# Later places for the transposes of the probabilities and the output products in a hybrid decoder layer

## The chip, the cores and the metric

The kernel runs on one core of a Trainium2 chip. The metric is the device time of one execution in microseconds, of which the median over several runs is compared. A profile of one execution shows every instruction of the engines: TensorE (PE, with its weight loads as PEld), VectorE (DVE), ScalarE (ACT), GpSimd (POOL) and SyncE (SP), which issues the weight transfers.

## The reference

One decoder layer on 256 positions of width 2048, all in float32. A projection gives a recurrent branch, a gating branch, 32 query heads on four key/value heads of size 64, and two merge gates. Attention looks at a window of 128 positions and has a sink in the denominator. After it come the merge, an output projection and an MLP of width 8192 with a squared ReLU. Cut to what matters here:

```python
h = rmsnorm(x, norm_mix_pre[l])
proj = h @ w_in[l]
xr, yr, q, k, v, g_rnn, g_attn = jnp.split(proj, IN_OFFSETS, axis=-1)
...
y_rnn = xr * jax.nn.gelu(yr)
q = rope(q.reshape(B, S, N_Q_HEADS, HEAD_DIM), positions)
k = rope(k.reshape(B, S, N_KV_HEADS, HEAD_DIM), positions)
y_att = sliding_window_sink_attention(q, k, v, attn_sinks[l])
mix = jax.nn.sigmoid(g_rnn) * (y_rnn @ w_rnn_proj[l]) + jax.nn.sigmoid(g_attn) * (y_att @ w_attn_proj[l])
x = x + rmsnorm(mix @ w_out[l], norm_mix_post[l])
h = rmsnorm(x, norm_mlp_pre[l])
u = jnp.square(jax.nn.relu(h @ w_mlp_up[l]))
x = x + rmsnorm(u @ w_mlp_down[l], norm_mlp_post[l])
...
# in the attention
m = jnp.maximum(jnp.max(scores, axis=-1, keepdims=True), sink)
p = jnp.exp(scores - m)
denom = jnp.sum(p, axis=-1, keepdims=True) + jnp.exp(sink - m)
probs = (p / denom).astype(v.dtype)
out = jnp.einsum('bnhgqk,bnkhd->bnqhgd', probs, vv)
```

## The kernel before, in words

**The weight stream.** All weights pass once, in one order, as halves of 128 x 1024 floats (`Stream`, L54). SyncE loads a half (L76), ScalarE casts it to a high part (`whi`, L94), VectorE subtracts to get the low part (`wlo`, L95), and TensorE makes float32 products from three products of parts. There are four raw buffers (`WRAW`) and six for each part (`WHALF`); a call of `ws.half()` splits up to six halves ahead, so the cast that it issues goes into the buffer of the half that TensorE has just finished.

**The passes.** `b_pass512` (L300) takes eight halves for one product of 256 rows by 512 columns: per half two steps, per step and row block three matmuls (L294, L296, L298), 12 matmuls a half and 96 a pass. `a_pair` (L243) takes four halves for two blocks of output channels, in turned form (L254, L256).

**The fill-in work.** Attention does not have a stage of its own. `waiting` is a list of generators; `pump()` (L227) resumes the first of them up to its next `yield`. `b_pass512` pumps after every `every` halves, `a_pair` four times in its four halves. So each `yield` in a generator marks one place among the matmuls of a pass.

**The order of the passes.** For each of four head groups g: a pass for the attention's merge gate (`g`, L646, which pumps after each half), then a pass for the queries (`q`, L648). The generator `attention(g)` (L532) is appended behind the query pass and so is resumed during the gate pass and the query pass of the next group; that of the last group during the first four `a_pair` passes of the recurrent branch (`recur(0)`, L765: two `conv`, two `gelu`), with `pump(99)` (L781) for what is left.

**The steps of `attention(g)`.** Rotary embedding of row block 0; transposes of the queries of block 0 and embedding of block 1; transposes of block 1; scores of both blocks, and the softmax of block 0; the softmax of block 1; `turn_probs(0)`; an empty step; `turn_probs(1)`; then the product with the values and its split into `yatt` (L626 to L635). `softmax(tb)` (L571) has nine exponentials on ScalarE (L578, L582, each of the latter followed by a row that reads its sum) and on VectorE a sum, a reciprocal and the division (L587), two instructions for block 0 and four for block 1. `turn_probs(tb)` (L592) makes two banks of four transposes for block 0 and four banks for block 1 (L604), each copied by ScalarE (L606). The pool `psm` from which these banks come has two. The product has 12 rows on TensorE (L630), two casts on ScalarE (L634) and two subtractions on VectorE (L635).

**What sets the order.** Within an engine a scheduler of the framework orders the recorded instructions; those under `pin` (the scores and the product matmuls) keep the program's order among themselves.

Of the kernel before, what the change touches and what calls it, by code (L numbers as in the profile page):

```python
# [28 lines left out]
TB = 2  # L29
# [137 lines left out]
def layer(tc, x, g_pre, pos_t, pos_row, inv_freq, vecs, sinks, gains, w_kv, w_q, w_xy, w_rg, w_g, w_rp, w_ap, w_out,  # L167
# [43 lines left out]
    def unit(name, dt=F32R):  # L211
        return big.tile([P, 4, 2, S], dt, tag="U8", name=name)

    def flat(t):
        return t.rearrange("p a b c -> p (a b c)")
# [3 lines left out]
    def units(name):  # L219
        return [unit(f"{name}{i}") for i in range(4)]  # L220

    def bank(pool, name):
        return pool.tile([P, 512], F32, tag=pool.name, name=name)

    waiting = []

    def pump(n=1):  # L227

        for _ in range(n):
            while waiting:  # L230
                try:
                    next(waiting[0])
                    break
                except StopIteration:
                    waiting.pop(0)
# [50 lines left out]
    def b_step(banks, acts, kt, hi, lo, last, tbs=(0, 1)):  # L286

        a = acts[kt // 4][:, kt % 4]
        first = kt == 0
        nb = len(banks[tbs[0]])  # L290
        for tb in tbs:
            t = slice(tb * P, tb * P + P)
            for n in range(nb):
                mm(banks[tb][n], a[:, 0, t], hi[:, n * 512 : n * 512 + 512], start=first, stop=False)  # L294
            for n in range(nb):
                mm(banks[tb][n], a[:, 0, t], lo[:, n * 512 : n * 512 + 512], start=False, stop=False)  # L296
            for n in range(nb):
                mm(banks[tb][n], a[:, 1, t], hi[:, n * 512 : n * 512 + 512], start=False, stop=last)  # L298

    def b_pass512(acts, banks, every=2):  # L300

        for j in range(8):
            hi, lo = ws.half()
            for i in range(2):
                c = slice(i * 512, i * 512 + 512)
                b_step([[b] for b in banks], acts, 2 * j + i, hi[:, c], lo[:, c], 2 * j + i == KT - 1)
            if (j + 1) % every == 0:
                pump()
        return banks

    def two_banks(name):
        room = pair(name)
        return [room[:, tb].rearrange("p a b -> p (a b)") for tb in range(TB)]
# [7 lines left out]
    psb = ctx_ps.enter_context(tc.tile_pool(name="psb", bufs=2, space=bass.MemoryType.PSUM))  # L321
# [45 lines left out]
    hT = units("hT")  # L367
# [164 lines left out]
    def attention(g, banks):  # L532
# [38 lines left out]
        def softmax(tb):  # L571
            stat = stats[tb]
            w = P * (1 + tb)
            per = 512 // w
            nc.vector.tensor_tensor(stat[:, 0, :], stat[:, 0, :], sk, ALU.max)
            nc.vector.tensor_scalar(stat[:, 1, :], stat[:, 0, :], -1.0, None, ALU.mult)
            nc.vector.tensor_tensor(stat[:, 2, :], sk, stat[:, 1, :], ALU.add)
            nc.scalar.activation(stat[:, 2, :], stat[:, 2, :], AF.Exp)  # L578
            for s3, at in tiles[tb]:
                for i in range(per):  # L580
                    c = slice(at + i, at + i + 1)
                    nc.scalar.activation(s3[:, i, :], s3[:, i, :], AF.Exp, bias=stat[:, 1, c],  # L582
                                         accum_out=stat[:, 3, c])
            nc.vector.tensor_tensor(stat[:, 2, :], stat[:, 2, :], stat[:, 3, :], ALU.add)
            nc.vector.reciprocal(stat[:, 2, :], stat[:, 2, :])
            for s3, at in tiles[tb]:
                nc.vector.tensor_tensor(s3, s3, stat[:, 2, at : at + per].unsqueeze(2).to_broadcast([P, per, w]),  # L587
                                        ALU.mult)
# [3 lines left out]
        def turn_probs(tb):  # L592
            nk = 1 + tb
            per = 4 // nk
            if tb:
                room_p = flat(unit("pT", F32)).rearrange("p (n c) -> p n c", c=512)
            else:
                room_p = rooms[tb][:, 2:4, :]
            for par in range(2):
                for kb in range(nk):  # L600
                    ps = bank(psm, "pt")
                    for h in range(4):
                        s3, at = tiles[tb][h // per * 2 + par]
                        nc.tensor.transpose(ps[:, h * P : h * P + P], s3[:, h % per, kb * P : kb * P + P], ident)  # L604
                    t = room_p[:, par * nk + kb, :]
                    nc.scalar.copy(t, ps)  # L606
                    pT[tb, par, kb] = t
# [9 lines left out]
        if last_group:  # L617
            scores(1, 1, [bank(psb, "sc") for par in range(2)])
        softmax(1)
        yield  # L620
        turn_probs(0)
        yield
        yield
        turn_probs(1)
        yield
        for tb in range(TB):  # L626
            po = bank(psm, "po")
# [16 lines left out]
    for g in range(NKV):  # L644
        m1.append(pa.tile([P, TB, 512], F32, tag="m1", bufs=4, name=f"m1{g}"))
        for tb, b in enumerate(b_pass512(hT, two_banks("g"), 1)):  # L646
            nc.scalar.activation(m1[g][:, tb], b, AF.Tanh, scale=r0h[tb])
        waiting.append(attention(g, b_pass512(hT, [bank(psb, f"q{tb}") for tb in range(TB)])))  # L648


    lam = vec[:, 7, :]
# [182 lines left out]
    psb = ctx2.enter_context(tc.tile_pool(name="psb2", bufs=4, space=bass.MemoryType.PSUM))  # L834
# [166 lines left out]
    for tb in range(TB):  # L1001
        for i in range(2):
            q = 2 + i
# [145 lines left out]
    for f in range(2):  # L1149
# [3 lines left out]
        for p in range(PAIRS):  # L1153
# [11 lines left out]
            if f == 1 or p >= R2_AT:  # L1165
                for q, u in full:
                    if q in SEVEN:
                        uT[q] = pc.tile([P, 2, 7, P], F32R, tag="seven", bufs=len(SEVEN), name=f"seven{f}{q}")
                    else:
                        i = sum(k not in SEVEN for k in range(q))  # L1170
# [137 lines left out]
```

## Time and profile before

| | |
|---|---|
| median of three runs | 1514.89 us |
| lowest and highest run | 1511.7 and 1516.5 us |
| span of the profiled execution | 1515.7 us |
| mean granted TensorE clock | 0.998 |
| transposes of the probabilities (L604), all groups | 96 rows, 14.13 us busy between 97 and 292 us |
| stage of the gate and query passes and `recur(0)` | about 45 to 298 us |

The page gives no time of the profiled execution beyond its span. The rows of a timeline give start and length in microseconds, engine, line, operation, the tiles written and read, the shape, how many equal instructions are merged, and in brackets the idle time of that engine before the row and what ended it. Lengths of matmuls overlap their successors, so costs on TensorE are read from start to start. `pt` is a bank of transposed probabilities, `s` the room of scores and probabilities, `po` the bank of the product, `q`, `g` and `ps` the banks of the passes.

### The profile page before, as it was taken

Reading aid. Unit: us, or ns where it says so; the run is one execution under the profiler, and the core shown is the slowest. Engines: PE = TensorE matmul, PEld = TensorE weight load, DVE = VectorE, ACT = ScalarE, POOL = GpSimd, SP = SyncE. Lnnn points to the kernel's source line nnn. Section 1 sums busy time; section 2 is a strip of 40 time slices with the busy share of each in tenths; the row PEclk is TensorE's granted clock in tenths of the full one; section 3 lists DMA queues with packets and bytes.
Section 4 is the critical chain, followed back from the end, with each engine's and each line's share of the span. In section 5 each row is a group of like instructions: output and inputs, shape, how many; then the busy total and the mean of one; then the engine's idle time right before and its main releaser. Section 6 shows DMA issues by size and latency. Waiting matters only on the chain.

```text
span 1515.7 us, 20016 instructions
## 1 busy us (share of the span) xinstructions
PE 1493.5 (99%) x7600; PEld 1259.8 (83%) x7600; DVE 1102.2 (73%) x1377; ACT 829.2 (55%) x1143; POOL 5.5 (0%) x11
## 2 busy tenths in 40 slices
PE   9999999999999999999999999999999999999996
PEld 7787778788888888888888888888888888888875
DVE  6666677858769966555667866798886666688897
ACT  6554654646566766443355655555454455555543
POOL 0000000000000000000000000000000000000001
PEclk9999999999999999999999999999999999999999
DMA  6645445465646565655764756566657555566564
GB/s 253 218 144 187 142 131 170 153 196 166 217 159 215 174 209 196 191 183 194 268 225 137 271 183 193 185 203 213 219 195 239 194 188 188 193 236 213 195 209 174
DMA packets 82895, 296.19 MB, mean 195 GB/s; under 512 B 9712, under 2 KB 9968, under 8 KB 81648
## 3 DMA queue, kind: packets, MB, share of 16 engines
q1 hardware_dynamic: 79056, 284.43, 57.4%
q10 hardware_dynamic: 3744, 10.50, 1.9%
q8 instruction: 59, 0.97, 0.2%
q14 instruction: 36, 0.29, 0.1%
HBM read 288.60 MB, written 6.29 MB: 195 GB/s over the span
## 4 chain that ended last, share of the span: by engine, by line
PE 82%; DVE 9%; DMA 4%; ACT 2%; issue 2%; DVEq 0%; SPq 0%; ACTq 0%
PE ps L256 21%; PE ps L254 11%; PE dQ L1084 4%; DMA wraw<-in_w_dn 4%; PE pp L294 4%; PE pp L296 4%; PE pp L298 4%; PE g L294 3%; DVE wlo L95 3%; PE g L298 3%; PE g L296 3%; PE s L1084 3%; PE dP L1084 2%; PE q L296 2%; PE q L298 2%; PE q L294 2%
## 5 line engine op out<-in xcount | busy, mean ns | idle before, releaser
L94 ACT CAST whi<-wraw 128x1024 fp32r<-128x1024 f32 x523 | 544.6, 1053 | 567.5 <-PE ps L256 123.7
L95 DVE TENSOR_TENSOR wlo<-wraw,whi 128x1024 fp32r<-128x1024 f32 x523 | 632.8, 1221 | 301.9 <-ACT whi L94 295.2
L256 PE MATMUL ps<-h2T,whi 128*128 128x512 f32 x960 | 223.9, 390 | 0.0
L256 PEld LDWEIGHTS ps<-h2T,whi 128*128 128x128 f32 x960 | 178.2, 188 | 35.6
L256 PE MATMUL ps<-hT,whi 128*128 128x512 f32 x512 | 121.3, 391 | 0.0
L254 PEld LDWEIGHTS ps<-h2T,wlo 128*128 128x128 f32 x960 | 119.1, 192 | 2.3
L254 PE MATMUL ps<-h2T,wlo 128*128 128x256 f32 x960 | 119.9, 283 | 0.0
L256 PEld LDWEIGHTS ps<-hT,whi 128*128 128x128 f32 x512 | 94.7, 188 | 20.1 <-issue 1.5
L1084 PE MATMUL dQ<-whi,uT 128*128 128x512 f32 x288 | 106.9, 389 | 0.0
L294 PE MATMUL g<-whi,hT 128*128 128x512 f32 x256 | 101.2, 395 | 0.0
L296 PE MATMUL g<-wlo,hT 128*128 128x512 f32 x256 | 100.0, 391 | 0.1
L298 PE MATMUL g<-whi,hT 128*128 128x512 f32 x256 | 99.8, 390 | 0.0
L254 PE MATMUL ps<-hT,wlo 128*128 128x256 f32 x512 | 64.9, 283 | 0.0
L254 PEld LDWEIGHTS ps<-hT,wlo 128*128 128x128 f32 x512 | 63.8, 191 | 1.2
L1084 PEld LDWEIGHTS dQ<-whi,uT 128*128 128x128 f32 x288 | 54.1, 188 | 11.2
L1084 PE MATMUL dQ<-wlo,uT 128*128 128x512 f32 x144 | 56.4, 391 | 1.2 <-DVE wlo L95 1.1
L294 PEld LDWEIGHTS g<-whi,hT 128*128 128x128 f32 x256 | 48.1, 188 | 10.6 <-issue 1.0
L298 PEld LDWEIGHTS g<-whi,hT 128*128 128x128 f32 x256 | 48.1, 188 | 10.2
L296 PEld LDWEIGHTS g<-wlo,hT 128*128 128x128 f32 x256 | 48.1, 188 | 9.9 <-DVE wlo L95 0.5
L1084 PE MATMUL dCs<-whi,uT 128*128 128x512 f32 x144 | 54.1, 389 | 0.0
L1084 PE MATMUL dP<-whi,uT 128*128 128x512 f32 x144 | 54.1, 389 | 0.0
L130 DVE TENSOR_TENSOR tlo<-t,thi 128x1536 fp32r<-128x1536 f32 x28 | 49.2, 1756 | 5.5 <-ACT thi L129 5.3
(280 smaller groups left out, 2462.1 us busy)
## 6 DMA issues: line engine op xcount, KB each, us to landing
wraw<-in_w_up SPq DMA_DIRECT2D x128, 512.0 KB, 4.1
wraw<-in_w_dn SPq DMA_DIRECT2D x128, 512.0 KB, 4.8
wraw<-in_w_g SPq DMA_DIRECT2D x64, 512.0 KB, 4.7
wraw<-in_w_xy SPq DMA_DIRECT2D x64, 512.0 KB, 4.5
wraw<-in_w_q SPq DMA_DIRECT2D x32, 512.0 KB, 4.4
wraw<-in_w_ap SPq DMA_DIRECT2D x32, 512.0 KB, 4.6
wraw<-in_w_rp SPq DMA_DIRECT2D x32, 512.0 KB, 4.1
wraw<-in_w_out SPq DMA_DIRECT2D x32, 512.0 KB, 4.9
```

The source lines that it names most:

```text
L94: self.pin(self.nc.scalar.copy(hi, src))
L95: self.pin(self.nc.vector.tensor_tensor(lo, src, hi.bitcast(F32), ALU.subtract))
L130: v.tensor_tensor(lo, t, hi.bitcast(F32), ALU.subtract)
L254: mm(ps[:, f, 1, :], w, a[:, 0, :], start=False, stop=j == 1 and k == 7)
L256: mm(ps[:, f].rearrange("p a b -> p (a b)"), w, a.rearrange("p a b -> p (a b)"), start=kt == 0, stop=j == 3 and k == 7)
L294: mm(banks[tb][n], a[:, 0, t], hi[:, n * 512 : n * 512 + 512], start=first, stop=False)
L296: mm(banks[tb][n], a[:, 0, t], lo[:, n * 512 : n * 512 + 512], start=False, stop=False)
L298: mm(banks[tb][n], a[:, 1, t], hi[:, n * 512 : n * 512 + 512], start=False, stop=last)
L1084: mm(b, a[x], w[y], start=not begun and i == 0, stop=tail and i == 2)
```

## The change

In `attention`, four more empty steps stand between the softmax of block 1 and `turn_probs(0)`, and one more between `turn_probs(1)` and the product. The query pass pumps after each half and no longer after every second one.

```diff
@@ -617,11 +617,13 @@
         if last_group:
             scores(1, 1, [bank(psb, "sc") for par in range(2)])
         softmax(1)
-        yield
+        for i in range(5):
+            yield
         turn_probs(0)
         yield
         yield
         turn_probs(1)
+        yield
         yield
         for tb in range(TB):
             po = bank(psm, "po")
@@ -645,7 +647,7 @@
         m1.append(pa.tile([P, TB, 512], F32, tag="m1", bufs=4, name=f"m1{g}"))
         for tb, b in enumerate(b_pass512(hT, two_banks("g"), 1)):
             nc.scalar.activation(m1[g][:, tb], b, AF.Tanh, scale=r0h[tb])
-        waiting.append(attention(g, b_pass512(hT, [bank(psb, f"q{tb}") for tb in range(TB)])))
+        waiting.append(attention(g, b_pass512(hT, [bank(psb, f"q{tb}") for tb in range(TB)], 1)))
```

In steps of the list above: `turn_probs(0)` was the sixth resumption of a group's generator and is the tenth, `turn_probs(1)` was the eighth and is the twelfth, and the product was the ninth and is the fourteenth. In halves of weights: the two turns come four halves later, the product four later in groups 0 to 2 (from behind the second half of the query pass to behind the sixth) and five later in the last group (from the third `a_pair` pass into the fourth).

## The prediction

> **What bounds the kernel now.** I read the page's head first, then the windows by stage, then the waits of TensorE, and only then the timeline around the transposes of the probabilities.
>
> ```profile
> span 1515.7 us, 20016 instructions
> PE 1493.5 (99%) x7600; PEld 1259.8 (83%) x7600; DVE 1102.2 (73%) x1377; ACT 829.2 (55%) x1143; POOL 5.5 (0%) x11
> PE 82%; DVE 9%; DMA 4%; ACT 2%; issue 2%; DVEq 0%; SPq 0%; ACTq 0%
> ```
>
> TensorE is busy for 1493.5 of 1515.7 us, and 82% of the chain that ended last is TensorE's. A microsecond in which TensorE stands still in the middle of the program is therefore a microsecond of the total, unless a later stage takes it back. The windows (start and end, length, then busy time and count of TensorE, weight loads, VectorE, ScalarE, GpSimd, granted clock, DMA share, GB/s) show where it stands still:
>
> ```profile
> 176.00:215.00 39.00, 39.00 (x196) 32.01 (x195) 25.93 (x38) 15.39 (x24) 0.00 (x0) 1.00 0.55 168
> 215.00:231.00 16.00, 14.57 (x76) 9.93 (x75) 10.45 (x16) 14.52 (x39) 0.00 (x0) 1.00 0.41 129
> 292.00:800.00 508.00, 508.00 (x2543) 432.45 (x2542) 341.83 (x394) 279.49 (x354) 0.00 (x0) 1.00 0.61 199
> 1322.00:1500.00 178.00, 175.88 (x786) 144.42 (x785) 150.81 (x148) 90.95 (x94) 3.81 (x2) 1.00 0.63 212
> ```
>
> From 176 to 215 us and from 292 to 800 us nothing is lost. The 16 us in which group 2 turns its probabilities lose 1.43 us. The last down projection, 1322 to 1500 us, loses 2.12 us. The view of waits, for TensorE alone, names the loss in the attention (total, times, longest):
>
> ```profile
> PE pt L604 <- DVE s L587: 4.4, 3, 1.5
> ```
>
> The transposes wait for the division of the softmax (L587) on VectorE. Group 1 in the timeline of TensorE (start, length, what, idle before it); the gap from one start to the next is what counts, since the lengths overlap:
>
> ```profile
> 160.97 0.39 PE L294 MATMUL q<-whi,hT 128*128 128x512 f32 x1
> 162.78 1.23 PE L604 MATMUL pt<-ident,s 128*128 128x128 f32 x8 [1.42 <-DVE s L587]
> 163.76 0.47 PE L296 MATMUL q<-wlo,hT 128*128 128x512 f32 x1
> 164.07 0.39 PE L298 MATMUL q<-whi,hT 128*128 128x512 f32 x1
> ...
> 169.13 0.39 PE L298 MATMUL q<-whi,hT 128*128 128x512 f32 x1
> 169.36 1.03 PE L604 MATMUL pt<-ident,s 128*128 128x128 f32 x8
> 170.15 0.48 PE L294 MATMUL q<-whi,hT 128*128 128x512 f32 x1
> ```
>
> A projection matmul takes 0.23 us from start to start (169.13 to 169.36), eight transposes that wait for nothing take 0.79 (169.36 to 170.15), and the first matmul behind transposes takes 0.31 (163.76 to 164.07), 0.08 more than its fellows; I call that the return. Against this the first turn stands 1.81 us behind the one matmul ahead of it, which is 1.58 too many, and its eight take 0.98, 0.19 too many, because the second four wait for the second division. Together 1.77 us in this group.
>
> **The change part by part.** It puts the 24 transposes, six copies, twelve product matmuls, two casts and two subtractions of each group later among the matmuls of the next pass. It adds and removes none of them, issues no DMA, and in the changed program SyncE's queue has the order that it had. On TensorE the order for groups 0 to 2 becomes: 24 matmuls of the query pass, the eight transposes of block 0, 24 matmuls, eight of block 1, three matmuls, the other eight (in groups 1 and 2 as four, one matmul, four), some 20 matmuls, the product. The more frequent call from the query pass alone moves nothing else, since no other generator waits then.
>
> *The waits removed.* VectorE and ScalarE in group 1:
>
> ```profile
> 161.94 1.29 DVE L587 TENSOR_TENSOR s<-s,stat 128x512 f32<-128x512 f32 x2
> 165.98 2.50 DVE L587 TENSOR_TENSOR s<-s,stat 128x512 f32<-128x512 f32 x4
> 168.40 1.22 DVE L95 TENSOR_TENSOR wlo<-wraw,whi 128x1024 fp32r<-128x1024 f32 x1
> ...
> 165.41 1.05 ACT L606 COPY s<-pt 128x512 f32<-128x512 f32 x2
> 166.35 1.05 ACT L94 CAST whi<-wraw 128x1024 fp32r<-128x1024 f32 x1
> 167.31 1.26 ACT L647 ACTIVATE m<-g,st 128x512 f32<-128x512 f32 x2
> 168.46 1.06 ACT L606 COPY pT<-pt 128x512 f32<-128x512 f32 x2
> ```
>
> The divisions end at 163.23 and 168.48, that is 2.3 and 7.5 us after the query pass begins at 160.97. In the changed order block 0 is turned after 24 x 0.23 = 5.5 us and block 1 after 48 x 0.23 and the 0.87 of the first turn with its return, 11.9 us. Both divisions are over by 3 to 4 us, so the waits go in full. The same count for the others, first groups 0 and 2, then the last group, whose turns stand in the paired passes of the recurrence:
>
> ```profile
> 108.60 0.39 PE L294 MATMUL q<-whi,hT 128*128 128x512 f32 x1
> 109.06 1.23 PE L604 MATMUL pt<-ident,s 128*128 128x128 f32 x8
> 110.04 0.48 PE L296 MATMUL q<-wlo,hT 128*128 128x512 f32 x1
> ...
> 216.01 0.39 PE L294 MATMUL q<-whi,hT 128*128 128x512 f32 x1
> 217.83 1.23 PE L604 MATMUL pt<-ident,s 128*128 128x128 f32 x8 [1.43 <-DVE s L587]
> ```
>
> ```profile
> 268.38 1.32 PE L256 MATMUL ps<-hT,whi 128*128 128x512 f32 x5
> 271.25 0.63 PE L604 MATMUL pt<-ident,s 128*128 128x128 f32 x4 [1.54 <-DVE s L587]
> ...
> 272.30 0.48 PE L256 MATMUL ps<-hT,whi 128*128 128x512 f32 x1
> ...
> 278.31 2.19 PE L254 MATMUL ps<-hT,wlo 128*128 128x256 f32 x17
> 280.60 0.63 PE L604 MATMUL pt<-ident,s 128*128 128x128 f32 x4
> 280.99 0.96 PE L254 MATMUL ps<-hT,wlo 128*128 128x256 f32 x6
> 281.81 0.63 PE L604 MATMUL pt<-ident,s 128*128 128x128 f32 x4
> 282.19 0.84 PE L254 MATMUL ps<-hT,wlo 128*128 128x256 f32 x5
> 282.89 1.15 PE L604 MATMUL pt<-ident,s 128*128 128x128 f32 x8
> 283.79 0.72 PE L254 MATMUL ps<-hT,wlo 128*128 128x256 f32 x4
> ```
>
> Group 0: 0.46 - 0.23 = 0.23 before and 0.19 inside, 0.42, and 0.04 because two fours with two returns become one eight with one: 0.46. Group 2: 1.82 - 0.23 + 0.19 = 1.78. Last group: 2.87 us for five matmuls, 1.72 too many. Then 1.05 us for eight transposes and a matmul, against 0.79 + 0.31 in one piece: 0.05 worse. Then 17 short matmuls in 2.29 us, where six and a return take 0.82, so 0.12 each and 2.04 for 17: 0.25 too many. Last 0.39 + 0.38 + 0.90 and three returns, 1.91, against two eights and two returns, 1.74: 0.17. Together 2.09. The sum over the groups is 0.46 + 1.77 + 1.78 + 2.09 = 6.1 us.
>
> *The waits added.* The block-1 turn needs four banks and the pool has two, so its third bank waits for the copy of the first. Before, that copy stood right behind TensorE, which was the late one. In the changed order of groups 1 and 2 a cast of a weight half (L94) stands ahead of the copies on ScalarE, and this cast waits for the buffer that TensorE gives free with its 48th matmul, just ahead of the turn. Let P be the turn's start. The 48th matmul starts 0.23 earlier and is 0.39 long, so the cast starts at about P + 0.2, the next instruction follows 0.96 later (166.35 to 167.31), and the first copy (1.06 for two, 0.59 for one) ends at P + 1.74. TensorE wants the bank at 0.79 + 0.31 + 2 x 0.23 = P + 1.56. A release reached TensorE 0.20 us after the first division (161.94 + 0.64 to 162.78); for a copy I take 0.1 to 0.2. That is a wait of 0.3 us in each of the two groups. Is ScalarE there in time? Behind its last exponential at 165.41 stand cast, two tanh, two casts, two copies, two casts: 0.96 + 1.15 + 1.92 + 0.94 + 1.92 = 6.9, to 172.3. P is 160.97 + 11.9 = 172.9, and the last cast is released at 173.1. It is, by 0.8 us. In group 0 a different cast order leaves the copies free, and nothing waits. In the last group the copy of the pass that has just ended stands ahead:
>
> ```profile
> 271.91 1.26 ACT L606 COPY s<-pt 128x512 f32<-128x512 f32 x2 [2.81 <-PE pt L604]
> ...
> 274.66 0.59 ACT L283 COPY px<-ps 128x512 f32<-128x512 f32 x1 [0.54 <-PE ps L256]
> ```
>
> With such a copy of 0.48 start to start ahead, the bank copies end at about P + 1.3 and P + 1.75, while TensorE wants them at 1.1 and 1.8 plus any wait: 0.4 us. Added in all: 0.3 + 0.3 + 0.4 = 1.0. Bounds: nothing, if the copies come in time; 1.0 plus a cast of 0.96 in three groups, 3.9, if ScalarE is late.
>
> The row at 271.91 shows ScalarE idle for 2.81 us for the transposes with a cast right behind it, so it took its instructions in order. [...]
>
> *Costed at nothing.* The product moves with its 2.7 us. Its copies and casts lie beside projection matmuls on ScalarE and VectorE, which have 1.5 and 5.5 us free in the 16 us of group 2 above. The weight halves stay ahead: the low part of the query pass's fifth half is made at 168.40 and over at 169.6, and without the stalls TensorE would want it behind the second turn's first eight, at about 172.9 + 0.8 = 173.7, 4 us later; if that cover went, TensorE would wait there instead. Attention products of the last group end inside the fourth paired pass, and their first reader wants that group's share only in the seventh of eight halves that follow, some 16 us on.
>
> *The sum.* 6.1 - 1.0 = 5.1 us. The profiled execution's span of 1515.7 becomes 1510.6. No time around the span is given for it; the span lies 0.8 above the median of the runs, 1514.89 (1511.7 to 1516.5). From the median: **1509.8**.
>
> **The rivals.**
> A gain of at least 0.3%, 4.54 us, is about what a measurement of this kernel can tell from no change: below 1510.35 is faster, above 1519.43 slower.
>
> *The copies come in time.* The third bank is never late. For it: ScalarE's 0.8 us in hand. Against: the cast is tied to TensorE's 48th matmul. Time: 1514.9 - 6.1 = 1508.8.
>
> *ScalarE is a cast late.* The exponentials hold ScalarE longer than counted, so in three groups the bank copies come 0.96 later: 6.1 - 3.9 = 2.2, so 1512.7. For it: the reserve is only 0.8 us. Against: the same instructions ran at this pace before.
>
> *The last stage takes it back.* If weights there arrive at a pace of their own, 1514.9 remains. For it: the 2.12 us lost from 1322 to 1500, where VectorE is busy 150.81 of 178. Against: nothing there starts before TensorE's release of a buffer, so the stage should move as a whole.
> [...]
>
> *A half late, slower.* If a bank copy stands behind a cast whose buffer is free only after a half that itself stands behind the waiting transposes, TensorE and ScalarE wait in turn, and each group loses about a half: 12 x 0.23 = 2.8 us, 11.0 in all, against 6.1 gained: 1519.8. It decides from 10.6 / 4 = 2.65 us per group. Against: the casts ahead of the copies are released by matmuls that stand ahead of the transposes.
>
> **How the numbers follow.** Forecast 0.60, its own range 1508.5 to 1512 by the bounds above and the scatter of the runs, of which 0.42 lies below 1510.35 and 0.18 above. Copies in time 0.18, faster. A cast late 0.10 and the last stage 0.05, both within 0.3%. A half late 0.07, of which 0.06 slower and 0.01 within. So faster 0.60, same 0.34, slower 0.06. The range 1506.0 to 1514.5 takes in the copies in time with 3 us of scatter below, the forecast and the late cast; the last two cases are left out.
>
> **What would show it.** In the changed profile TensorE's wait for the division (4.4 us in three times) is gone, and the matmul ahead of block 0's turn is followed at 0.23. Waits of the third transpose bank for the copies show 0.3 to 0.4 in groups 1, 2 and the last. Windows over the same instructions are shorter by 0.46, 1.5, 1.5 and 1.7 us. The prediction is wrong if these windows shrink and the span does not, if TensorE waits for a low part in the query passes, or if the bank waits exceed a cast.

## The result, and the profile after

The changed kernel is slower. Its median is 1518.86 us (1515.52 to 1522.69, 13 runs) beside 1514.73 for the kernel before (1511.7 to 1516.5, 13 runs): a ratio of 1.0026 with a 95% interval of 1.0019 to 1.0034, 4.1 us more. That is inside the 0.3% that the text ahead called no change, but the interval leaves no doubt of the sign. 1509.8 was forecast, and the range ended at 1514.5.

The head of the page of the changed kernel, and its chain of waits by engine:

```profile
span 1520.9 us, 20016 instructions
PE 1494.9 (98%) x7600; PEld 1262.8 (83%) x7600; DVE 1101.0 (72%) x1377; ACT 829.3 (55%) x1143; POOL 5.5 (0%) x11
PE 89%; DVE 5%; DMA 3%; ACT 2%; issue 1%; SPq 0%; DVEq 0%; ACTq 0%
```

The same 7600 matmuls keep TensorE busy as long as before to within 1.4 us, so most of the time came as waits, not as work. The profiled execution took 1522.69 us, 1.8 more than its span, and is the slowest of its runs; that is why lengths of stretches are compared below, and medians for the whole. The view of waits for TensorE (total, times, longest) has one row of the transposes left:

```profile
PE pt L604 <- ACT pT L606: 9.3, 4, 3.7
```

The wait for the division, 4.4 us in three times, is gone. In its place the transposes wait for the copies that empty their banks, 9.3 us. The timeline of TensorE in group 1 of the changed kernel shows one such place:

```profile
172.63 0.39 PE L298 MATMUL q<-whi,hT 128*128 128x512 f32 x1
172.86 1.03 PE L604 MATMUL pt<-ident,s 128*128 128x128 f32 x8
...
174.20 0.40 PE L298 MATMUL q<-whi,hT 128*128 128x512 f32 x1
178.30 0.66 PE L604 MATMUL pt<-ident,s 128*128 128x128 f32 x4 [3.71 <-ACT pT L606]
...
181.20 0.63 PE L296 MATMUL q<-wlo,hT 128*128 128x512 f32 x1
181.63 0.63 PE L298 MATMUL q<-whi,hT 128*128 128x512 f32 x1
...
185.75 1.08 PE L632 MATMUL po<-s,v_sb 128*64 128x512 f32 x4
```

Block 1's turn starts at 172.86 behind its predecessor by 0.23 us, without a wait, just where the prediction put it (172.9). Then its third bank comes 4.1 us after the matmul ahead of it. ScalarE over the same stretch:

```profile
167.59 1.99 ACT L94 CAST whi<-wraw 128x1024 fp32r<-128x1024 f32 x2
169.48 1.07 ACT L606 COPY s<-pt 128x512 f32<-128x512 f32 x2
170.43 1.06 ACT L94 CAST whi<-wraw 128x1024 fp32r<-128x1024 f32 x1
173.66 1.05 ACT L94 CAST whi<-wraw 128x1024 fp32r<-128x1024 f32 x1 [2.17 <-DMA wraw<-in_w_g]
176.72 1.04 ACT L94 CAST whi<-wraw 128x1024 fp32r<-128x1024 f32 x1 [2.01 <-DMA wraw<-in_w_g]
177.67 1.07 ACT L606 COPY pT<-pt 128x512 f32<-128x512 f32 x2
```

The bank copies, ready to run from about 173.5, stand behind two casts that each wait some 2 us for a weight half which is still on its way. In the kernel before, the same copies ran at 168.46 and 170.35, and in the view of ScalarE's waits from 155 to 190 us no cast there is held last by a load: its casts wait for TensorE to free a buffer, 2.2 us at the longest. Why the halves are late is in the chain of waits of the changed kernel (start, length, what):

```profile
164.61 0.99 ACT s L582 x4
165.60 0.94 ACT whi L94
166.54 1.05 ACT m L649 x2
...
167.59 2.00 ACT whi L94 x2
...
169.62 1.22 DVE wlo L95
...
170.86 5.76 DMA wraw<-in_w_g
...
176.72 1.04 ACT whi L94
177.76 0.49 ACT pT L606
```

Read it backwards: the copy waited for a cast, the cast for a load of 5.76 us, the load for a raw buffer, the buffer for the low part that VectorE made at 169.62, and this for the second of the two casts that ScalarE began at 167.59, behind its exponentials (L582, over at 165.6), another cast and two tanh (L649). Of the two late loads the chain goes through the second alone. SyncE's queue in the kernel before shows that the pause was there already (start, length from the first issue to the last, count):

```profile
146.35 13.57 SPq L76 DMA_DIRECT2D wraw<-in_w_q  x4
169.64 17.99 SPq L76 DMA_DIRECT2D wraw<-in_w_g  x8
```

Between 160 and 169.6 us no weight half is requested (in the changed kernel until 169.7): all four raw buffers are full, because the softmax holds the two engines that empty them; 9.6 us is SyncE's longest wait for a low part in either kernel between 150 and 175 us. So the pause is old; the change moved the copies from before its consequences to behind them.

The windows of the changed kernel (start and end, length, busy time and count of TensorE, weight loads, VectorE, ScalarE, GpSimd, clock, DMA share, GB/s) add one thing:

```profile
172.80:178.30 5.50, 1.79 (x12) 1.25 (x10) 2.03 (x3) 2.63 (x4) 0.00 (x0) 1.00 0.88 285
178.30:187.00 8.70, 8.70 (x35) 6.42 (x37) 2.01 (x3) 3.80 (x6) 0.00 (x0) 0.80 0.40 142
```

Behind the stall the granted clock is 0.80 over these 8.70 us (0.50 in a window from 179 to 182 us), and the matmuls at 181.20 and 181.63 follow each other by 0.43 us, not 0.23. The stall's price has a second part that no wait shows.

To set kernel against kernel I measured four stretches of TensorE, each from the first matmul of one pass to the first of a later one, over the same instructions: the query pass behind group 0, 1 and 2 each, and the recurrent branch with the last group. For group 1 that is 160.97 to 190.20 before and 161.05 to 194.07 changed.

| stretch, us | before | changed | difference |
|---|---|---|---|
| group 0 | 27.92 | 28.57 | +0.65 |
| group 1 | 29.23 | 33.02 | +3.79 |
| group 2 | 29.24 | 32.91 | +3.67 |
| last group | 56.58 | 55.74 | -0.84 |
| sum | | | +7.27 |

### The profile page after: what moved, and what is told of

It reads as the page before. It is cut to its first block, busy times and chain, and to the rows that moved or that the text cites. A ratio compares the mean times of both kernels' runs of the same rounds, so it can differ in the third digit from the quotient of the medians.

```text
span 1520.9 us, 20016 instructions
## 1 busy us (share of the span) xinstructions
PE 1494.9 (98%) x7600; PEld 1262.8 (83%) x7600; DVE 1101.0 (72%) x1377; ACT 829.3 (55%) x1143; POOL 5.5 (0%) x11
## 4 chain that ended last, share of the span: by engine, by line
PE 89%; DVE 5%; DMA 3%; ACT 2%; issue 1%; SPq 0%; DVEq 0%; ACTq 0%
PE ps L256 22%; PE ps L254 12%; PE dQ L1086 7%; PE pp L294 4%; PE pp L296 4%; PE pp L298 4%; PE s L1086 4%; PE g L294 4%; PE g L296 4%; PE g L298 4%; PE dP L1086 3%; PE dCs L1086 2%; DMA wraw<-in_w_dn 2%; PE o L296 2%; PE o L298 2%; PE o L294 2%
## 5 line engine op out<-in xcount | busy, mean ns | idle before, releaser
L256 PE MATMUL ps<-h2T,whi 128*128 128x512 f32 x960 | 223.9, 390 | 0.0
L256 PEld LDWEIGHTS ps<-h2T,whi 128*128 128x128 f32 x960 | 178.2, 188 | 35.6
L256 PE MATMUL ps<-hT,whi 128*128 128x512 f32 x512 | 121.0, 391 | 0.0
L256 PEld LDWEIGHTS ps<-hT,whi 128*128 128x128 f32 x512 | 94.7, 188 | 19.4 <-issue 0.7
```

The lines of the kernel that those rows point to most:

```text
L256: mm(ps[:, f].rearrange("p a b -> p (a b)"), w, a.rearrange("p a b -> p (a b)"), start=kt == 0, stop=j == 3 and k == 7)
```

## The experiments

The theory: the gain in the turns is real, and it is lost because block 1's third and fourth bank wait for copies that stand on ScalarE behind casts that wait for late loads (ready from about 173.5, the first pair in group 1 began at 177.67). The rivals: the loss comes from the products or the weight halves (the low part, or the half itself, late for TensorE), from the later last stage, or from the turn's position as such. Ratios are against the kernel before in runs beside it.

**Four banks for block 1 in the query passes.** The copies stay where they are behind the casts, but TensorE no longer needs them inside the turn:

```diff
+            more = two_banks("pt") if tb and not last_group else None
...
-                    ps = bank(psm, "pt")
+                    ps = more[kb] if more and par else bank(psm, "pt")
```

with the four copies issued behind the four banks.

> The changed kernel, with the places of all steps kept, but in groups 0 to 2 the four banks of block 1's transposes come from two pools (two banks of the small pool, two of a pair that is free in the query pass), so no transpose waits for a copy of an earlier one. Queue theory (the copies stand on ScalarE behind casts that wait for a weight half's landing, and TensorE waits for the copies): the waits of TensorE for these copies (9.3 us in the changed kernel) fall under 1 us, the granted clock in groups 1 and 2 stays at 1.00, the stretch from query pass to next pass falls from 33.0 to about 27.7 us in each of the two, and the median falls by 9 to 11 us to 1508 to 1510. Starvation theory (the weights themselves are late, and TensorE would stand still a little later in any case): the wait moves to the weight loads or low parts of the halves that follow, and the median stays at 1516 to 1519.

Measured: 1508.72 us beside 1513.72, a ratio of 0.9965 (0.9952 to 0.9977). The stretches are 27.40, 27.42, 27.42 and 55.78: 4.95 us less than before in sum. ScalarE of this kernel in group 1, and TensorE's turn:

```profile
172.94 1.04 ACT L94 CAST whi<-wraw 128x1024 fp32r<-128x1024 f32 x1 [2.19 <-DMA wraw<-in_w_g]
175.11 1.05 ACT L94 CAST whi<-wraw 128x1024 fp32r<-128x1024 f32 x1 [1.13 <-DMA wraw<-in_w_g]
176.07 2.04 ACT L615 COPY pT<-pt 128x512 f32<-128x512 f32 x4
```

```profile
172.10 1.91 PE L607 MATMUL pt<-ident,s 128*128 128x128 f32 x16
173.76 0.48 PE L294 MATMUL q<-whi,hT 128*128 128x512 f32 x1
```

The casts still wait for the loads, and the copies still come 4 us after the turn's start; but all 16 transposes run in one piece and nobody waits. So neither products nor weight halves nor the position are the loss: it is that the turn has two banks while their copies are late. The last group, which has two banks in this kernel too, keeps one wait of 1.1 us for a copy.

**The second turn one half earlier.** One `yield` instead of two between the turns, three instead of two behind the second.

> The changed kernel with the turn of block 1 one weight half behind that of block 0 instead of two, and the product one later, so that it stays where it was put. Queue theory: one cast fewer, or two, stands ahead of the copies, and the last of these needs no load that was held up by the softmax; TensorE's waits for the copies fall from 9.3 us to under 3, none over 1.5, the granted clock stays at 1.00, and the median is 1509 to 1512. Starvation theory: the waits come back at the low parts of later halves, 1516 to 1519. If being late as such costs the time (the product's place, more things in the query pass): no change from 1519.

Measured: 1511.76 beside 1513.72, ratio 0.9982 (0.9973 to 0.9992); stretches 27.66, 28.31, 28.32 and 56.49. The waits of TensorE, and ScalarE in group 1:

```profile
PE pt L604 <- ACT pT L606: 1.7, 3, 0.6
PE pt L604 <- ACT s L606: 1.1, 1, 1.1
```

```profile
170.73 1.06 ACT L94 CAST whi<-wraw 128x1024 fp32r<-128x1024 f32 x1
171.68 1.07 ACT L606 COPY pT<-pt 128x512 f32<-128x512 f32 x2
174.01 1.05 ACT L94 CAST whi<-wraw 128x1024 fp32r<-128x1024 f32 x1 [1.26 <-DMA wraw<-in_w_g]
```

Twelve matmuls, 2.8 us, lie between slower and faster: with the first pair of copies ahead of the casts that wait for a load, the longest wait for block 1's copies falls from 3.7 to 0.6 us. The second row, a wait of 1.1 us for a copy of block 0, is in the last group.

**The change in the outer groups alone.** Groups 0 and 3 as changed, groups 1 and 2 with the single `yield` ahead of the first turn as before.

```diff
-        for i in range(5):
+        late = g in (0, NKV - 1)
+        for i in range(5 if late else 1):
```

> The change in the first and the last head group alone; groups 1 and 2 turn and multiply where they did before. Queue theory: groups 1 and 2 take 29.2 us each again (33.0 and 32.9 in the changed kernel), so 7.5 us of the loss go and the median comes to 1511 to 1515, the same as before the change or a little faster. If the loss is spread or comes from elsewhere (the last group, the pump after each half): 1516 to 1519.

Measured: 1512.43 beside 1513.72, ratio 0.9993 (0.9984 to 1.0002), no difference; stretches 28.45, 29.23, 29.21 and 55.78, 0.3 us less than before in sum. Groups 1 and 2 are back at their times of before, so these two hold the loss.

**Block 1's division on GpSimd.** If VectorE is free for the low parts during the softmax, raw buffers come free earlier and the loads start earlier; the change else as it is.

```diff
-                nc.vector.tensor_tensor(s3, s3, stat[:, 2, at : at + per].unsqueeze(2).to_broadcast([P, per, w]),
-                                        ALU.mult)
+                (nc.gpsimd if tb and g < NKV - 1 else nc.vector).tensor_tensor(
+                    s3, s3, stat[:, 2, at : at + per].unsqueeze(2).to_broadcast([P, per, w]), ALU.mult)
```

> The changed kernel with the division of block 1's probabilities on GpSimd in groups 0 to 2, so that VectorE can make the low parts behind the softmax up to 1.9 us earlier, raw buffers come free earlier and the held loads start earlier. Queue theory: the two loads on which the last casts ahead of the copies wait start 1 to 1.9 us earlier, and TensorE's wait of 3.7 us in groups 1 and 2 shrinks by 1 to 2.7 us each; the median is 1512 to 1517. If the copies are late because of the place among TensorE's matmuls (the cast tied to the buffer that TensorE frees): the wait stays at 3.6 to 3.8 us and the median at 1518 to 1520.

Measured: 1517.31 beside 1513.72, ratio 1.0020 (1.0010 to 1.0029); stretches 29.20, 31.19, 29.69 and 55.77, 2.9 us more than before in sum instead of 7.3. Group 0 became slower than with the change alone: there the first copies now stand behind both casts that wait for a load, and the third bank waits 1.48 instead of 0.83 us. The median lies 0.3 us above what was expected. ScalarE, VectorE with GpSimd, and a low part and the load in the chain of waits, in group 1:

```profile
172.46 1.05 ACT L94 CAST whi<-wraw 128x1024 fp32r<-128x1024 f32 x1 [0.62 <-DMA wraw<-in_w_g]
175.24 1.04 ACT L94 CAST whi<-wraw 128x1024 fp32r<-128x1024 f32 x1 [1.73 <-DMA wraw<-in_w_g]
176.19 1.07 ACT L606 COPY pT<-pt 128x512 f32<-128x512 f32 x2
```

```profile
166.91 1.81 DVE L95 TENSOR_TENSOR wlo<-wraw,whi 128x1024 fp32r<-128x1024 f32 x1 [0.53 <-ACT whi L94]
169.00 6.79 DVE L95 TENSOR_TENSOR wlo<-wraw,whi 128x1024 fp32r<-128x1024 f32 x4 [0.28 <-ACT whi L94]
176.31 1.23 DVE L95 TENSOR_TENSOR wlo<-wraw,whi 128x1024 fp32r<-128x1024 f32 x1 [0.52 <-ACT whi L94]
166.60 6.99 POOL L587 TENSOR_TENSOR s<-s,stat 128x512 f32<-128x512 f32 x4 [48.11 <-ACT s L582]
```

```profile
169.00 1.71 DVE wlo L95
...
170.73 4.41 DMA wraw<-in_w_g
```

The casts wait 2.35 us for loads instead of 4.18, which is 1.83 less, and the stall of this group is 1.89 us instead of 3.71, which is 1.82 less; the longest of the kernel is 2.0. The lateness of the loads does set the size of the stall. The remedy is a half one. Of the low parts that VectorE began while GpSimd divided (166.60 to 173.59), those at 166.91 and 169.00 took 1.81 and 1.71 us; the four of the row above, which ends 2.20 us behind GpSimd, took 6.79, where four in a row take 4.62 in the changed kernel (168.49 to 173.11). The one at 176.31, behind GpSimd, took 1.23, and 1.22 is the mean of the changed kernel. So the load that matters began only 0.13 us earlier (170.73 and 170.86), 0.5 counted from the start of the pass, where 1 to 1.9 were expected; it was over sooner mostly because it took 4.41 instead of 5.76 us. Why it did stays open.

**The second turn three halves later.** Five `yield`s between the turns instead of two, one behind instead of two.

> The changed kernel with the turn of block 1 moved later still, behind the seventh half of the query pass, and the product behind the eighth (in the last group, correspondingly, to the end of its four paired passes). Still two banks. Queue theory: by then the loads that the softmax held up have landed, so the casts ahead of the copies wait for no load; TensorE's waits for the copies fall from 9.3 us to 1 to 2.5 us, none over 1, with some 0.5 to 1 us more where the product now stands close behind the last copies; granted clock 1.00; median 1509 to 1513. If being later costs in itself, or two banks are simply too few wherever the turn stands: waits of 3 us or more remain and the median is 1517 to 1522.

Measured: 1513.92 beside 1513.54, ratio 1.0004 (0.9995 to 1.0012); stretches 28.10, 27.59, 27.58 and 59.25. In the query passes it did what it should: by then the loads have nearly caught up (the waits of the casts for them in group 1 fall from 2.15 to 0.24 us), and the third bank waits some 0.2 us in groups 1 and 2 and 0.6 in group 0. The last group spoils it, which was not expected, and the median lies above the 1509 to 1513 that were. TensorE and ScalarE there:

```profile
293.71 1.14 PE L604 MATMUL pt<-ident,s 128*128 128x128 f32 x8 [3.02 <-ACT pT L606]
```

```profile
289.60 1.05 ACT L94 CAST whi<-wraw 128x1024 fp32r<-128x1024 f32 x1 [1.88 <-PE pt L604]
290.56 0.63 ACT L711 ACTIVATE u<-py 128x512 f32<-128x512 f32 x1
292.55 0.63 ACT L713 ACTIVATE xct<-u 128x512 f32<-128x512 f32 x1 [1.37 <-DVE u L712]
293.08 1.05 ACT L606 COPY pT<-pt 128x512 f32<-128x512 f32 x2
```

It is the same trap with another bait: the copies stand behind an activation of the recurrent branch (L713) that waits for VectorE, and TensorE waits 3.02 us with them. Here too TensorE is slow behind the stall: twelve matmuls (L256) from 294.61 to 299.12 us take 0.38 each from start to start, where six of the same kind from 283.77 to 285.13 take 0.23.

**Four banks in every group.** As in the first experiment, and in the last group two banks from the other pool.

> The kernel of the four-bank run with four banks in the last group too (there the second two come from the pool of the query banks, which is idle then). Queue theory: the 1.1 us that TensorE still waited for a copy in the last group go, because the copies no longer gate a transpose; the last group's stretch from its first paired pass to the attention projection falls from 55.8 to about 54.7 us, and the median is 1507 to 1509. If the wait only moves to the product: 55.8 us again and 1508 to 1510.

Measured: 1506.77 beside 1513.54, ratio 0.9956 (0.9943 to 0.9968), the fastest kernel here; stretches 27.42 three times and 54.32, 6.4 us less than before. The window of the stretch of the last group, with TensorE busy from end to end:

```profile
240.95:295.27 54.32, 54.32 (x334) 45.75 (x332) 48.11 (x96) 34.85 (x72) 0.00 (x0) 1.00 0.46 151
```

TensorE does not stand still in the attention any more, and no row of the transposes is left among its waits.

**The changed kernel once more,** unaltered, beside the last two.

> The changed kernel as it is, for a second profile, since its first one is the slowest of its runs (1522.69 against a median of 1518.86), and lost 7.3 us up to the attention projection where the median lost 4.1. If the loss in the attention varies with the landing times of the held loads: this profile shows waits for the copies other than 9.3 us, and 4 to 6 us lost up to the attention projection in a run nearer the median. If it is fixed: again 7.0 to 7.5 us lost there, and the last down projection gives some back. Queue theory allows both; the median is 1517 to 1520.

Measured: 1519.4 beside 1513.54, ratio 1.0042 (1.0026 to 1.0057); stretches 28.51, 32.51, 32.54 and 55.76, 6.35 us more than before. The loss is there in two profiled executions, 7.3 and 6.35, with stalls of 3.7 and 3.5 us as the longest.

## Why the prediction was wrong, step by step

**The waits removed: right.** With four banks nothing takes the gain back, and its size can be read: 27.92 - 27.42 = 0.50, 29.23 - 27.42 = 1.81, 29.24 - 27.42 = 1.82 and 56.58 - 54.32 = 2.26, together 6.4 us, where 0.46, 1.77, 1.78 and 2.09, together 6.1, were worked out. The gain also arrives in full at the end: 1513.54 - 1506.77 = 6.8 us between medians.

**The waits added: the step that failed.** The prediction asked the right question, "Is ScalarE there in time?", and answered "It is, by 0.8 us". That count added up durations of instructions and let the last cast wait only for the buffer "that TensorE gives free with its 48th matmul". A cast has a second input, the raw half. Two of the casts ahead of the copies waited 2.17 and 2.01 us for it, and the copies began at 177.67 instead of the 174.1 that this step implies (173.1 and a cast). What was to be "a wait of 0.3 us in each of the two groups" became 3.7 and 3.6, and with that the sign of being wrong that the prediction gave itself, "if the bank waits exceed a cast". Where the loads had nearly caught up, in the kernel with the second turn three halves later, the 0.3 of the forecast was met in these two groups: some 0.2.

The same gap stands in "The weight halves stay ahead", which looked at when low parts are made and not at when the next half is requested. The two rows of SyncE's queue above would have shown it in the profile of before: no request between 160 and 169.6 us. Add a load, 5.76 us in the chain of waits above and 4.7 from issue to landing in the median of `in_w_g` on the page of before, and a cast wanted at 171 to 173 cannot run.

**The upper bound of the added waits, 3.9 us, was too small.** It took ScalarE to be late by one cast, its own work. The actual lateness, in both middle groups, was that of a load (5.76 and 5.67 us long in the chain of waits), and behind the stall came a slower clock (0.80 from 178.3 to 187.0 us in group 1). Group 1 by parts, against the four banks' 27.42: the third bank starts 4.10 us after its predecessor instead of 0.23, so 3.87; the 20 matmuls up to the product at 185.75, the first of them at 0.43, take 1.3 more; of what remains of the 5.6 us, about 0.4, most is the slower clock as well: the last four transposes take 0.71 us from start to start (179.07 to 179.78), where four took 0.38 in the kernel before.

**Group 0 and the last group.** "In group 0 a different cast order leaves the copies free" was wrong as well: group 0 lost 0.65 where it was to gain 0.46, with a wait of 0.83 us for copies that stood behind a cast which waited 2.34 us for its half. In the last group 0.84 was gained with two banks, 2.26 with four; 1.4 of added wait, not 0.4, and part of it a cast that waited 0.31 us for its half.

**The rivals.** "ScalarE is a cast late" had the right engine and under a third of the size: 3.9 us, where 13.7 lie between the stretches of the changed kernel and of four banks everywhere. "A half late, slower" is nearest in time (1519.8) and names the right picture, TensorE and ScalarE waiting in turn behind a cast, with 2.8 us per group; but it has the cast wait for TensorE, and that was not what happened. It got a chance of 0.07, argued away by "the casts ahead of the copies are released by matmuls that stand ahead of the transposes": the same neglected input. "The last stage takes it back" isn't borne out. From the first matmul of the attention projection to the last one of the program it is 1203.1 us before and 1201.6 in the first profile of the changed kernel, but 1199.5 in its repetition and in both kernels with four banks. In the last down projection TensorE waits 2.1 us before, 1.3 changed, and in those three not at all, though the repetition arrives there late and the other two early. Between the repetition and four banks everywhere 12.7 us of the stretches are 12.6 between the medians, so nothing is taken back. Against the kernel before the total isn't settled as finely: it has one profile, whose extra 3.5 us behind the attention are not explained, and the loss of 7.3 or 6.35 us in the attention shows as 4.1 and 5.9 in the medians, the gain of 6.4 as 6.8.

## What to carry to other kernels

When an instruction is moved to a later place, list what now stands ahead of it on each engine that serves it, and for each of these ask for all its inputs, the transfers too; sums of durations did not show here the waits of 2.17 and 2.01 us for loads that were harmless where they stood. A copy that empties a bank for TensorE should not stand behind a prefetch, which cost TensorE up to 3.7 us in one place here; where it must, give the producer as many banks as one burst needs, which here turned 0.42% slower (the changed kernel's repetition) into 0.44% faster. Look for the pauses in the transfer queue behind a softmax or another burst, and for what is placed behind them: here the pause from 160 to 169.7 us was followed by the two waiting casts, the second of which began at 176.72.

## What the runs showed of the hardware beyond that

**The clock behind the stalls.** After each of the four stalls of 3.29 to 3.71 us in groups 1 and 2 of the changed kernel's two profiles TensorE ran at about half its pace. The second four transposes behind the stall took 0.71 us from start to start, where four took 0.38 in the kernel before, and in three of the four cases matmuls followed each other by 0.43 (rows above for one of them). The granted clock of the first profile was 0.50 from 179 to 182 us and from 237 to 240. The 0.23 us were back 2.9 to 4.2 us behind the end of the stall. After the one of 3.02 us in the last group of the kernel with the second turn three halves later, twelve matmuls took 0.38 each. The waits of 1.42 to 1.54 us in the kernel before and of 0.6 in the kernel with the earlier second turn left the 0.23 as it was. In between it is open: in the kernel with the division on GpSimd a stall of 1.89 us in group 1 was followed by the slow pace and one of 2.01 us in group 2 was not. Their rows:

```profile
176.82 0.66 PE L604 MATMUL pt<-ident,s 128*128 128x128 f32 x4 [1.89 <-ACT pT L606]
...
178.97 0.63 PE L294 MATMUL q<-whi,hT 128*128 128x512 f32 x1
179.40 0.63 PE L296 MATMUL q<-wlo,hT 128*128 128x512 f32 x1
```

```profile
233.94 0.66 PE L604 MATMUL pt<-ident,s 128*128 128x128 f32 x4 [2.01 <-ACT pT L606]
...
235.57 0.40 PE L294 MATMUL q<-whi,hT 128*128 128x512 f32 x1
235.81 0.39 PE L296 MATMUL q<-wlo,hT 128*128 128x512 f32 x1
```

What set the two cases apart is not shown by these runs.

**VectorE beside GpSimd.** Two low parts that began while GpSimd divided took 1.71 and 1.81 us, and four in a row, the first of them at 169.00, 6.79; in the changed kernel one takes 1.22 in the mean and four in a row 4.62. What slowed them is not shown by these runs.
